# Gate projection as one level of Strassen's product over pairs of token tiles

## The chip, the cores and the metric

One core of one Trainium2 chip runs the whole layer in a single launch. The metric is device microseconds (us) of one execution; lower is better. Times of a kernel are medians of several executions.

## The reference, cut to what matters

One encoder layer over 1024 tokens with model width 1024. After the two attention branches the reference ends like this:

```python
y = jnp.einsum('bse,ed->bsd', jnp.concatenate([ya, yb], axis=-1), w_out[i])
x = x + y
gate = jax.nn.sigmoid(jnp.einsum('bsd,de->bse', x, w_ple_gate[i]))
x = x + gate * jnp.einsum('bsp,pd->bsd', p[i], w_ple_proj[i])
```

The product with `w_ple_gate` (1024 x 1024 by 1024 x 1024) is the gate product; it is the last matrix product of the kernel. Every float32 operand of a large product is split into a high and a low part, and a product is the sum of three matmuls: high by high, high by low, low by high.

## The kernel before, in words

**Tiling.** Tokens come in 8 tiles of 128 rows. A tile of `x1` (the residual stream after the output projection) is 128 x 1024. Matmuls are 128x128 stationary by 128x512 moving. The work of each engine is issued in the order of the program text; every engine and the DMA queue of SyncE (SP, all loads and stores of this part) work strictly in that order.

**The end of the attention and the output projection.** The loop over `i` (lines 1339 to 1383) runs the differential attention; its last turns are i = 33 to 37. `outb` (line 1015) adds branch B's share of the output projection and stores it to DRAM as `xpd`. `outa(t)` (line 1219) loads tile t of `xpd`, makes 24 matmuls into a two-bank PSUM tile, and VectorE adds the two (line 1233). `outa(0)` to `outa(4)` are issued in turns 33 to 37 (line 1330), `outa(5)` to `outa(7)` in the loop behind (lines 1384 to 1395). Between them lies the rest of the attention for the last query pair (pair 15): `d_f` and `d_f2` (lines 1159 to 1175: one VectorE operation, then six short ones on GpSimd), `d_fb` (line 1177, transposes on TensorE, behind `outa(4)`), `d_y` (line 1185: VectorE line 1190, ScalarE line 1195, GpSimd line 1196).

**The gate.** `load_wg` and `split_wg` (lines 1203 to 1214) load and split the weights, 8 rows of 128x1024, once. For each token tile `x1_trans` (line 1236) transposes the tile on TensorE (8 transposes), and ScalarE and VectorE make the two parts. `gate(t)` (line 1249) makes 48 matmuls, 24 for each half of 512 columns; then a tanh on ScalarE (line 1263), two VectorE operations (lines 1264, 1265) and a store. The gate runs one tile behind the transposes, and the last three `outa` are threaded between the first gates.

**Buffers.** SBUF pools: `T8` (16 of 8 KB), `T4` (8 of 4 KB), `TA` (6 of 4 KB), `T2`/`T15` (11 of 2 KB). PSUM has 8 banks: `PS` hands out 4 single banks, `PS2` two tiles of two banks. A new tile waits until all readers of the tile that had its buffer are done.

Of the kernel before, what the change touches and what calls it, by code (L numbers as in the profile page):

```python
# [15 lines left out]
P = 128  # L16
D = 1024
# [23 lines left out]
def layer_kernel(ctx, tc, x, p, ngr, w_in, w_out, gains, lamv, t5p, rpbp, w_gate, w_ple,  # L41
                 onehot, pen, sel, out):
    nc = tc.nc
# [95 lines left out]
    idn = CT([P, P], n="idn")  # L139
# [148 lines left out]
    ppd = [DT([P, D], n="ppd") for _ in range(8)]  # L288
# [388 lines left out]
    pts = {}  # L677
# [282 lines left out]
    for i in range(len(steps) + 2):  # L960
# [8 lines left out]
        if got:  # L969
            n, t0, c = got  # L970
# [31 lines left out]
    xpd = [DT([P, D], n="xpd") for _ in range(8)]  # L1002
# [196 lines left out]
    wgh = []
    wgl = []  # L1200
    wgr = {}

    def load_wg(kc):
        wgr[kc] = T4([P, D], n="wgr")
        ld(wgr[kc], w_gate[kc * P:(kc + 1) * P, :])

    def split_wg(kc):
        if kc % 2 == 0:
            wgh.append(T8([P, 2, D], F32R, n="wgh"))
            wgl.append(T8([P, 2, D], F32R, n="wgl"))  # L1210
        r = wgr.pop(kc)
        h, l = wgh[kc // 2], wgl[kc // 2]
        act(h[:, kc % 2], r, AF.Copy)
        zl.append(lambda: V.tensor_tensor(l[:, kc % 2], r, h.bitcast(F32)[:, kc % 2], op=OP.subtract))
# [21 lines left out]
    def x1_trans(t):
        xt = x1[t]
        h = T4([P, 8, P], F32R, n="x1h")
        l = T4([P, 8, P], F32R, n="x1l")
        for g in range(2):  # L1240
            tp = PS([P, 4, P], "x1p")
            for k in range(4):
                kc = 4 * g + k
                nc.tensor.transpose(tp[:, k], xt[:, kc * P:(kc + 1) * P], idn)
            act(h[:, 4 * g:4 * g + 4], tp, AF.Copy)
            V.tensor_tensor(l[:, 4 * g:4 * g + 4], tp, h.bitcast(F32)[:, 4 * g:4 * g + 4], op=OP.subtract)
        x1T[t] = (h, l)

    def gate(t):
        h, l = x1T.pop(t)  # L1250
        xt = x1.pop(t)
        for c in range(2):
            cs = slice(c * 512, c * 512 + 512)
            pp = T2([P, 512], n="ppl")
            ld(pp, ppd[t][:, cs])
            ps = PS([P, 512], "gps")
            for k in range(8):
                wh, wl = wgh[k // 2][:, k % 2, cs], wgl[k // 2][:, k % 2, cs]
                mm(ps, h[:, k], wh, start=(k == 0), stop=False)  # L1259
                mm(ps, h[:, k], wl, start=False, stop=False)  # L1260
                mm(ps, l[:, k], wh, start=False, stop=(k == 7))  # L1261
            th = T2([P, 512], n="gth")
            act(th, ps, AF.Tanh, scale=0.5)
            V.scalar_tensor_tensor(th, th, 1.0, pp, op0=OP.add, op1=OP.mult)
            V.tensor_tensor(xt[:, cs], th, xt[:, cs], op=OP.add)
            ld(out[t * P:(t + 1) * P, cs], xt[:, cs])
# [72 lines left out]
    for i in range(1, NI + 6):  # L1339
        pre_d(i)  # L1340
        if i == 1 or i == 2:
            load_wout(1, i + 1)
        if i == 28 or i == 31:
            for k in range(2):
                load_wout(0, k + 2 * (i == 31))
        even = i % 2 == 0
        pv = (i - 4) // 2
        if even and i < NI:
            load_u(i // 2)
        for m in range(2):  # L1350
            if i < NI:
                d_e(i, m)
            if 0 <= i - 3 + m < NI:
                d_l(i - 3 + m, 1 - m)
            if m == 0 and 0 < i <= NI:
                d_a(i - 1)
            if even:
                if 0 <= (i - 6) // 2 < NP and m == 0:
                    d_f((i - 6) // 2)
                    d_f2((i - 6) // 2)  # L1360
                filler(i, m)
                if 0 <= pv < NP:
                    d_pv(pv, 4 * m)
            else:
                if 0 <= (i - 7) // 2 < NP and m == 1:
                    d_y((i - 7) // 2)
                if 0 <= (i - 5) // 2 < NP and m == 0:
                    d_pv2((i - 5) // 2)
                filler(i, m)
            if i + 1 < NI:  # L1370
                d_s(i + 1, m)
            if 0 <= i - 2 < NI:
                d_t(i - 2, m)
            if not even and m == 0 and 0 <= (i - 7) // 2 < NP:
# [4 lines left out]
        if i >= 34:
            for kc in (2 * (i - 34), 2 * (i - 34) + 1):  # L1380
                load_wg(kc)
                if i > 34:
                    split_wg(kc - 2)
    for t in range(5, 8 + 6):
        z_low()
        if t == 5:
            split_wg(6)
            z_low()
            split_wg(7)
        if 0 <= t - 5 < 8:  # L1390
            x1_trans(t - 5)
        if t >= 6:
            gate(t - 6)
        if t < 8:
            outa(t)
# [63 lines left out]
```

## Time and profile before

| what | value |
|---|---|
| median of 3 executions | 829.63 us (827.16 to 831.23) |
| the profiled execution, own time | 825.45 us |
| its span in the profile | 823.7 us |
| TensorE (PE) busy | 781.7 us, 95% of the span |
| VectorE (DVE), ScalarE (ACT), GpSimd (POOL) busy | 514.6, 437.2, 261.3 us |
| mean granted TensorE clock | 0.984 of full |

The span runs from the first to the last instruction of the profiled execution; 1.75 us of that execution's time lie around it. PE is the matmul pipe, PEld the weight loads that overlap it, SPq the queue of SyncE. Matmuls overlap in the pipe, so that the time between two starts (not the 390 ns of one) is what a matmul costs.

### The profile page before, as it was taken

Reading aid. Unit: us, or ns where it says so; the run is one execution under the profiler, and the core shown is the slowest. Engines: PE = TensorE matmul, PEld = TensorE weight load, DVE = VectorE, ACT = ScalarE, POOL = GpSimd, SP = SyncE. Lnnn points to the kernel's source line nnn. Section 1 sums busy time; section 2 is a strip of 40 time slices with the busy share of each in tenths; the row PEclk is TensorE's granted clock in tenths of the full one; section 3 lists DMA queues with packets and bytes.
Section 4 is the critical chain, followed back from the end, with each engine's and each line's share of the span. In section 5 each row is a group of like instructions: output and inputs, shape, how many; then the busy total and the mean of one; then the engine's idle time right before and its main releaser. Section 6 shows DMA issues by size and latency. Waiting matters only on the chain.

```text
span 823.7 us, 12188 instructions
## 1 busy us (share of the span) xinstructions
PE 781.7 (95%) x4242; PEld 647.9 (79%) x4242; DVE 514.6 (62%) x990; ACT 437.2 (53%) x814; POOL 261.3 (32%) x263
## 2 busy tenths in 40 slices
PE   7999899999989999797989988999999999999997
PEld 6788688888878887576867867888888877888886
DVE  4658976786997675445536568777777743732332
ACT  5765545254444545335635578888888852311120
POOL 1001433352655400011101035777777752100000
PEclk9999999999999999999989999999999999999999
DMA  8855363862889997585767578667577427122222
GB/s 318 321 199 185 120 212 101 283 156 85 237 262 239 239 307 198 142 232 164 213 174 194 168 219 231 169 173 209 162 211 192 161 96 281 77 89 91 93 87 90
DMA packets 118541, 151.94 MB, mean 184 GB/s; under 512 B 23848, under 2 KB 76744, under 8 KB 118352
## 3 DMA queue, kind: packets, MB, share of 16 engines
q1 hardware_dynamic: 116688, 145.39, 58.9%
q0 software_dynamic: 1792, 5.77, 2.1%
q8 instruction: 34, 0.56, 0.3%
q14 instruction: 27, 0.22, 0.1%
HBM read 104.96 MB, written 46.17 MB: 183 GB/s over the span
## 4 chain that ended last, share of the span: by engine, by line
PE 65%; DMA 11%; DVE 11%; ACT 5%; issue 3%; SPq 3%; POOL 2%; DVEq 0%; ACTq 0%; POOLq 0%
PE dsp L1066 6%; PE ips L234 6%; PE ips L236 6%; PE ips L235 6%; PE gps L1261 4%; PE gps L1259 4%; PE gps L1260 4%; DMA Vw<-vb 3%; PE dtp L1108 3%; SPq L97 2%; PE ntp L685 2%; DMA wraw<-in_w_in_dram 2%; PE dpv L1135 2%; PE zps L582 2%; PE zps L584 2%
## 5 line engine op out<-in xcount | busy, mean ns | idle before, releaser
L234 PE MATMUL ips<-w,xh 128*128 128x512 f32 x336 | 134.0, 399 | 3.6 <-DVE C L260 3.0
L236 PE MATMUL ips<-w,xl 128*128 128x512 f32 x336 | 131.8, 392 | 0.0
L235 PE MATMUL ips<-w,xh 128*128 128x512 f32 x336 | 131.3, 391 | 0.0
L1091 POOL TENSOR_TENSOR s<-s,s 128x1024 f32<-128x1024 f32 x32 | 77.1, 2408 | 57.0 <-ACT s L1090 55.3
L433 POOL TENSOR_TENSOR qrs<-qms,nhalf 128x16 f32<-128x16 f32 x16 | 51.4, 3214 | 91.1 <-DVE qms L431 91.1
L1076 DVE CUSTOM_DVE_ANT_0 s<-dsp,T 128x1024 f32<-128x1024 f32 x64 | 77.7, 1215 | 2.5 <-PE dsp L1066 2.5
L234 PEld LDWEIGHTS ips<-w,xh 128*128 128x128 f32 x336 | 63.4, 189 | 17.1 <-issue 3.8
L1078 ACT ACTIVATE s<-s,dm 128x1024 f32<-128x1024 f32 x64 | 73.3, 1146 | 4.6 <-DVE dm L1076 4.5
L1066 PE MATMUL dsp<-K,Q 128*128 128x512 f32 x256 | 69.7, 394 | 4.9 <-DVE dm L1076 4.3
L236 PEld LDWEIGHTS ips<-w,xl 128*128 128x128 f32 x336 | 63.4, 189 | 13.8
L1115 DVE TENSOR_TENSOR aTl<-dtp,aTh 128x512 fp32r<-128x512 f32 x64 | 44.2, 691 | 48.0 <-ACT aTh L1109 48.0
L235 PEld LDWEIGHTS ips<-w,xh 128*128 128x128 f32 x336 | 63.6, 189 | 12.7
L716 POOL TENSOR_TENSOR yb<-nay,yb 128x128 fp32r<-128x128 f32 x32 | 16.4, 514 | 168.8 <-ACT yb L715 168.8
L218 DVE TENSOR_TENSOR w<-wraw,w 128x512 fp32r<-128x512 f32 x84 | 62.2, 778 | 5.6 <-ACT w L217 5.5
L687 ACT ACTIVATE PT<-ntp 96x768 f32<-96x768 f32 (+1 forms) x32 | 25.9, 810 | 63.0 <-PE ntp L685 63.0
L1066 PEld LDWEIGHTS dsp<-K,Q 128*128 128x128 f32 x256 | 45.9, 189 | 14.6 <-issue 3.1
L582 PE MATMUL zps<-xh,zw 128*128 128x512 f32 x128 | 54.2, 423 | 0.0
L584 PE MATMUL zps<-xh,zw 128*128 128x512 f32 x128 | 51.3, 401 | 0.0
L583 PE MATMUL zps<-xl,zw 128*128 128x512 f32 x128 | 51.1, 399 | 0.0
L217 ACT ACTIVATE w<-wraw 128x512 fp32r<-128x512 f32 x84 | 48.4, 626 | 4.7 <-DVE wraw L193 4.7
L1109 ACT ACTIVATE aTh<-dtp 128x512 fp32r<-128x512 f32 x64 | 38.0, 593 | 23.8 <-PE dtp L1108 23.7
L1259 PE MATMUL gps<-wgh,x1h 128*128 128x512 f32 x128 | 50.5, 395 | 0.0
(177 smaller groups left out, 1820.9 us busy)
## 6 DMA issues: line engine op xcount, KB each, us to landing
wraw<-in_w_in_dram SPq DMA_DIRECT2D x72, 256.0 KB
x<-in_x_dram SPq DMA_DIRECT2D x8, 512.0 KB
ppd<-pp SPq DMA_DIRECT2D x8, 512.0 KB
K<-kbh SPq DMA_DIRECT2D x8, 512.0 KB
Q<-qbh SPq DMA_DIRECT2D x16, 256.0 KB
Q<-qah SPq DMA_DIRECT2D x16, 256.0 KB
Q<-qal SPq DMA_DIRECT2D x16, 256.0 KB
wor<-in_w_out_dram SPq DMA_DIRECT2D x8, 512.0 KB
```

Of the source, the lines that this page charges most:

```text
L218: V.tensor_tensor(w[:, 1], r, w.bitcast(F32)[:, 0], op=OP.subtract)
L234: mm(ps, lh[:, k, a:a + P], w[:, 0], start=(new and k == 0), stop=False, skip_group_check=cont)
L235: mm(ps, lh[:, k, a:a + P], w[:, 1], start=False, stop=False, skip_group_check=cont)
L236: mm(ps, ll[:, k, a:a + P], w[:, 0], start=False, stop=(k == 3), skip_group_check=cont)
L433: G.tensor_tensor(rs, ms, nhalf, op=OP.pow)
L582: mm(ps, w[:, 0, kc], xh(kc, a, b), start=(kc == 0), stop=False)
L584: mm(ps, w[:, 1, kc], xh(kc, a, b), start=False, stop=(kc == 7))
L1066: mm(ps[:, cs], q[g][:, m, u * P:(u + 1) * P], k[:, cs], start=(g == 0), stop=(g == 1))
L1076: V.tensor_tensor_reduce(out=s, in0=ps, in1=back(Td[h][:, :], 1919 - (896 - P * qt), [[-1, S]]), scale=-1.0, scalar=BIG, op0=OP.add, op1=O ...
L1078: act(s, s, AF.Exp, bias=mx, scale=-1.0, accum_out=z[:, m:m + 1])
L1091: G.tensor_tensor(s1, s1, s2, op=OP.add)
L1259: mm(ps, h[:, k], wh, start=(k == 0), stop=False)
```

## The change

The gate product is computed for pairs of token tiles (p, p + 4) as a 2 x 2 block product with seven products in place of eight (the Winograd form of Strassen). The four quarters of the weights give seven right operands: B11, B21, B22 and the sums T1 to T4; the two token tiles give seven left operands: A11, A12, A22 and S1 to S4. Products P1, P6, P7, P4 accumulate in one PSUM bank (A), P5 and P3 in another (B), P2 in a third (C), and partial sums are copied out between them. In detail:

- `gate(p)` makes 7 products of 12 matmuls for two tiles. Tile pair 0's transposes and splits (`g_left1` to `g_left3`) stand between the last three `outa`; pair p + 1's stand inside `gate(p)`.
- `g_first(k)` makes T1, T2 by two GpSimd subtractions for each of four rows k and splits B11, B21, T1, T2; it is issued at the ends of turns 35, 36, 37 and behind `outa(5)`. `g_second(k)` loads the quarters a second time and makes T3, T4 and B22's split; rows 0 and 1 are issued before the first gate, rows 2 and 3 (`extra(0)`) inside it behind P2, the split of T4 (`extra(1)`) behind P7.
- `outa(t)` loads the next tile's `xpd` before its own matmuls and now stores its sum back to `xpd`, one product late; only tiles 0 and 4 stay in SBUF, the others are loaded again in `gate`, and each half tile once more as the addend.
- The last three `outa` run ahead of the first gate.

```diff
...
+    GLEFT = dict(P1="A11", P2="A12", P6="S2", P5="S1", P7="S3", P3="S4", P4="A22")
+    GRIGHT = dict(P1="B11", P2="B21", P6="T2", P5="T1", P7="T3", P3="B22", P4="T4")
...
+    def g_split(n, k, r):
+        h, l = gw[n]
+        act(h[:, k], r, AF.Copy)
+        V.tensor_tensor(l[:, k], r, h.bitcast(F32)[:, k], op=OP.subtract)
+
+    def g_first(k):
+        a, b, c, d = [gr.pop((n, k)) for n in ("B11", "B12", "B21", "B22")]
+        G.tensor_tensor(b, b, a, op=OP.subtract)
+        g_split("B11", k, a)
+        g_split("B21", k, c)
+        G.tensor_tensor(d, d, b, op=OP.subtract)
+        g_split("T1", k, b)
+        g_split("T2", k, d)
+
+    def g_second(k):
+        a, b, c, d = [gr.pop((n, k)) for n in ("B11", "B12", "B21", "B22")]
+        V.tensor_tensor(b, d, b, op=OP.subtract)
+        g_split("T3", k, b)
+        G.tensor_tensor(a, a, b, op=OP.add)
+        G.tensor_tensor(c, c, a, op=OP.subtract)
+        g_split("B22", k, d)
+        gr["T4", k] = c
...
     def outa(t):
-        xt = TA([P, D], n="x1")
-        ld(xt, xpd[t])
+        if t not in oax:
+            outa_load(t)
+        xt = oax.pop(t)
+        if t < 7:
+            outa_load(t + 1)
+        flush()
         pss = PS2([P, D], "oap")
...
         V.tensor_tensor(xt, pss, xt, op=OP.add)
-        x1[t] = xt
...
+        late.append(lambda: st(xpd[t], xt))
+        if t % 4 == 0:
+            x1[t] = xt
...
+    def l_split(p, n, src):
+        w = T4([P, 2, 4, P], F32R, n="x1s")
+        gl[p, n] = w
+        act(w[:, 0], src, AF.Copy)
+        V.tensor_tensor(w[:, 1], src, w.bitcast(F32)[:, 0], op=OP.subtract)
+
+    def g_left1(p):
+        pa, pb = [PS2([P, 2, 4, P], "x1p") for _ in range(2)]
+        pts = [pa[:, 0], pa[:, 1], pb[:, 0], pb[:, 1]]
+        for i in range(4):
+            xt = x1[p + 4 * (i // 2)]
             for k in range(4):
...
+                kc = 4 * (i % 2) + k
+                nc.tensor.transpose(pts[i][:, k], xt[:, kc * P:(kc + 1) * P], idn)
...
+        act(f[:, 0], pts[0], AF.Copy)
+        act(f[:, 1], pts[1], AF.Copy)
+        act(e[:, 0], pts[2], AF.Copy)
+        V.tensor_tensor(e[:, 1], pts[3], e[:, 0], op=OP.add)
+        l_split(p, "A22", pts[3])
+        l_split(p, "A11", f[:, 0])
+        l_split(p, "A12", f[:, 1])
+        V.tensor_tensor(e[:, 0], f[:, 0], e[:, 0], op=OP.subtract)
+        l_split(p, "S1", e[:, 1])
+        V.tensor_tensor(e[:, 1], e[:, 1], f[:, 0], op=OP.subtract)
...
+    def gate(p, extra):
...
+        pre = [g_pre(p, 0), g_pre(q, 1)]
+        g_prod(p, A, "P1", True)
+        act(wv[:, 0], A, AF.Copy)
+        while last:
+            last.pop()()
+        if nxt:
+            x1_load(p + 1)
+            x1_load(q + 1)
+        flush()
+        g_prod(p, C, "P2", True)
+        th = T2([P, 512], n="gth")
+        V.tensor_tensor(th, C, wv[:, 0], op=OP.add)
+        extra(0)
+        g_prod(p, A, "P6", False)
+        act(xy[:, 0], A, AF.Copy)
+        g_fin(p, 0, th, pre.pop(0), th)
+        g_prod(p, B, "P5", True)
+        act(wv[:, 1], B, AF.Copy)
+        if nxt:
+            g_left1(p + 1)
+        pre += [g_pre(p, 1), g_pre(q, 0)]
+        flush()
+        g_prod(p, A, "P7", False)
+        act(xy[:, 1], A, AF.Copy)
+        th1 = T2([P, 512], n="gth")
+        V.tensor_tensor(th1, xy[:, 1], wv[:, 1], op=OP.add)
+        extra(1)
+        g_prod(p, B, "P3", False)
...
+        g_prod(p, A, "P4", False)
...
+        if i == 34:
+            g_load(0, QUARTERS)
+        if i >= 35:
+            if i == 35:
+                g_tiles("B11", "B21", "T1", "T2")
+            g_load(i - 34, QUARTERS)
+            g_first(i - 35)
+    z_low()
+    outa(5)
+    g_first(3)
+    g_left1(0)
+    g_load(0, QUARTERS)
+    outa(6)
+    g_left2(0)
+    g_left3(0)
+    g_load(1, QUARTERS)
+    outa(7)
+    flush()
...
+    def extra(j):
+        if j == 0:
+            g_second(2)
+            g_second(3)
+        else:
+            for k in range(4):
+                g_split("T4", k, gr.pop(("T4", k)))
+
+    g_second(0)
+    g_second(1)
+    for p in range(4):
+        gate(p, extra if p == 0 else lambda j: None)
...
```

In the diff `G` is GpSimd, `V` VectorE, `act` ScalarE. `g_prod` makes the 12 matmuls of a product, `g_pre` loads the two addends of a half tile, `g_fin` is the tanh, the two VectorE operations and a store that is issued late, `flush` issues the stores put off, and `g_left2`, `g_left3` split S2, S3 and S4.

## Rows read from the trace of the kernel before

**Rows 1.** The page, busy time of each engine.
```profile
PE 781.7 (95%) x4242; PEld 647.9 (79%) x4242; DVE 514.6 (62%) x990; ACT 437.2 (53%) x814; POOL 261.3 (32%) x263
```

**Rows 2.** Four stretches: length, busy (instructions) of PE, PEld, DVE, ACT, POOL; clock, DMA share, GB/s.
```profile
681.95:707.66 25.71, 25.71 (x130) 21.76 (x130) 9.90 (x13) 5.83 (x9) 7.84 (x15) 1.00 0.74 286
707.66:715.00 7.34, 7.34 (x43) 6.34 (x42) 5.91 (x7) 5.49 (x8) 0.74 (x1) 1.00 0.00 0
715.00:818.50 103.50, 103.50 (x481) 85.76 (x479) 34.17 (x49) 15.85 (x29) 0.00 (x0) 1.00 0.26 87
818.50:823.70 5.20, 0.00 (x0) 0.00 (x0) 1.38 (x2) 0.60 (x1) 0.00 (x0) 0.73 0.13 50
```

**Rows 3.** The first of the gate's matmul groups by line, 600 us to the end.
```profile
L1259 PE MATMUL gps<-wgh,x1h 128*128 128x512 f32 x128 | 50.5, 395 | 0.0
```

**Rows 4.** ACT in order of time: start, duration, operation, idle before and its releaser.
```profile
795.86 0.60 ACT L1263 ACTIVATE gth<-gps 128x512 f32<-128x512 f32 x1 [4.79 <-PE gps L1261]
796.35 1.09 ACT L1245 ACTIVATE x1h<-x1p 128x512 fp32r<-128x512 f32 x2
802.22 0.60 ACT L1263 ACTIVATE gth<-gps 128x512 f32<-128x512 f32 x1 [4.77 <-PE gps L1261]
807.66 0.60 ACT L1263 ACTIVATE gth<-gps 128x512 f32<-128x512 f32 x1 [4.84 <-PE gps L1261]
```

**Rows 5.** PE in order of time, around `outa(5)`.
```profile
707.66 1.04 PE L1244 MATMUL x1p<-idn,x 128*128 128x128 f32 x8
```

**Rows 6.** DVE and POOL in order of time, durations used for the chain of the change.
```profile
697.18 0.41 DVE L1190 TENSOR_TENSOR y<-oc,dfb 128x256 f32<-128x256 f32 x1
...
684.23 0.19 POOL L1168 TENSOR_TENSOR ft<-ft,drz 128x2 f32<-128x2 f32 x1
686.04 0.19 POOL L1174 TENSOR_TENSOR f<-f,ind 128x2 f32<-128x2 f32 x1
698.12 0.74 POOL L1196 TENSOR_TENSOR yal<-y,yah 128x256 fp32r<-128x256 f32 x1 [11.88 <-ACT yah L1195]
702.47 0.20 POOL L1174 TENSOR_TENSOR f<-f,ind 128x2 f32<-128x2 f32 x1
```

**Rows 7.** DVE and POOL in order of time, 225 to 230 and 249 to 256 us.
```profile
225.37 1.28 DVE L218 TENSOR_TENSOR w<-wraw,w 128x512 fp32r<-128x512 f32 x2
227.77 1.21 DVE L270 TENSOR_TENSOR C<-ips,X 128x1024 f32<-128x1024 f32 x1
251.63 3.46 DVE L218 TENSOR_TENSOR w<-wraw,w 128x512 fp32r<-128x512 f32 x2
...
227.55 2.54 POOL L179 TENSOR_TENSOR wraw<-wraw,wraw 128x512 f32<-128x512 f32 x2
249.33 6.92 POOL L182 TENSOR_TENSOR wraw<-wraw,wraw 128x512 f32<-128x512 f32 x4
```

**Rows 8.** A load of a tile of `xpd`: its issue on SP, and the DVE operation that waited.
```profile
730.20 0.32 SPq L97 DMA_DIRECT2D x<-xpd  x1
733.78 1.22 DVE L1233 TENSOR_TENSOR x<-oap,x 128x1024 f32<-128x1024 f32 x1 [5.70 <-DMA x<-xpd]
```

**Rows 9.** Stretches around three idle times of PE (columns as rows 2), and their ends.
```profile
418.00:430.00 12.00, 7.92 (x42) 6.31 (x39) 4.75 (x17) 2.51 (x7) 0.91 (x2) 0.72 0.56 167
660.00:668.00 8.00, 6.41 (x34) 5.76 (x34) 4.51 (x8) 6.80 (x10) 5.21 (x4) 0.79 0.25 88
679.00:683.00 4.00, 2.73 (x17) 2.14 (x16) 2.15 (x3) 1.21 (x3) 0.72 (x2) 1.00 0.00 1
...
422.26 1.51 PE L685 MATMUL ntp<-idn,nas 128*128 128x128 f32 x6 [4.08 <-DVE nas L675]
662.12 0.61 PE L1156 MATMUL dss<-ones,osq 128*128 128x1 f32 x4 [1.59 <-DVE aTl L1115]
681.48 0.61 PE L1156 MATMUL dss<-ones,osq 128*128 128x1 f32 x4 [1.27 <-DVE aTl L1115]
```

**Rows 10.** The page's second part for 680 to 700 us: GB/s in 40 slices of 0.5 us.
```profile
GB/s 0 0 0 0 0 0 0 0 0 0 287 303 115 377 238 188 426 385 418 442 401 426 401 426 426 418 426 418 418 418 410 418 418 401 401 418 410 410 401 418
```

More of the change, by code (lines that the diff above doesn't have):

```diff
@@ L1196, in d_y @@
         G.tensor_tensor(yl[:, h % 2, cs], y, yh.bitcast(F32)[:, h % 2, cs], op=OP.subtract)
[L1199 to L1214, printed above, removed]
+    GLEFT = dict(P1="A11", P2="A12", P6="S2", P5="S1", P7="S3", P3="S4", P4="A22")
@@ new lines, in layer_kernel, with g_load, g_tiles @@
+    GRIGHT = dict(P1="B11", P2="B21", P6="T2", P5="T1", P7="T3", P3="B22", P4="T4")
+    gw = {}
+    gr = {}
+    gl = {}
+    def g_load(k, names):
+        for n in names:
+            i, j = int(n[1]) - 1, int(n[2]) - 1
+            gr[n, k] = T2([P, 512], n="wgr")
+            ld(gr[n, k], w_gate[(4 * i + k) * P:(4 * i + k + 1) * P, j * 512:(j + 1) * 512])
+    def g_tiles(*names):
+        for n in names:
+            gw[n] = (T8([P, 4, 512], F32R, n="wgh"), T8([P, 4, 512], F32R, n="wgl"))
@@ L1216, in layer_kernel, with flush, outa_load @@
+    QUARTERS = ("B11", "B12", "B21", "B22")
     x1 = {}
     x1T = {}
-    def outa(t):
-        xt = TA([P, D], n="x1")
-        ld(xt, xpd[t])
+    oax = {}
+    late = []
+    def flush():
+        while late:
+            late.pop(0)()
+    def outa_load(t):
+        oax[t] = TA([P, D], n="x1")
+        ld(oax[t], xpd[t])
+    def outa(t):
+        if t not in oax:
[4 more added lines that the diff above has]
+        flush()
         pss = PS2([P, D], "oap")
@@ L1233, in outa @@
         V.tensor_tensor(xt, pss, xt, op=OP.add)
-        x1[t] = xt
[L1236 to L1241, printed above, removed]
-            for k in range(4):
[L1243 to L1266, printed above, removed]
+        late.append(lambda: st(xpd[t], xt))
@@ new lines, in outa, with x1_load @@
+        if t % 4 == 0:
+            x1[t] = xt
+    def x1_load(t):
+        x1[t] = TA([P, D], n="x1")
+        ld(x1[t], xpd[t])
+    lt = {}
+    def l_split(p, n, src):
[8 more added lines that the diff above has]
+            xt = x1[p + 4 * (i // 2)]
+            for k in range(4):
+                kc = 4 * (i % 2) + k
+                nc.tensor.transpose(pts[i][:, k], xt[:, kc * P:(kc + 1) * P], idn)
+        x1.pop(p)
+        x1.pop(p + 4)
+        f = TA([P, 2, 4, P], n="x1f")
+        e = TA([P, 2, 4, P], n="x1e")
+        lt[p] = (f, e)
+        act(f[:, 0], pts[0], AF.Copy)
[8 more added lines that the diff above has]
+        V.tensor_tensor(e[:, 1], e[:, 1], f[:, 0], op=OP.subtract)
@@ new lines, in g_left2, with g_left3, g_prod @@
+    def g_left2(p):
+        f, e = lt[p]
+        l_split(p, "S2", e[:, 1])
+        l_split(p, "S3", e[:, 0])
+        V.tensor_tensor(e[:, 1], f[:, 1], e[:, 1], op=OP.subtract)
+    def g_left3(p):
+        l_split(p, "S4", lt.pop(p)[1][:, 1])
+    def g_prod(p, ps, n, new):
+        w = gl.pop((p, GLEFT[n]))
+        h, l = gw[GRIGHT[n]]
+        c = not new
+        for k in range(4):
+            mm(ps, w[:, 0, k], h[:, k], start=(new and k == 0), stop=False, skip_group_check=c)
+            mm(ps, w[:, 0, k], l[:, k], start=False, stop=False, skip_group_check=c)
+            mm(ps, w[:, 1, k], h[:, k], start=False, stop=(k == 3), skip_group_check=c)
@@ new lines, in g_pre, with g_fin @@
+    def g_pre(t, c):
+        cs = slice(c * 512, c * 512 + 512)
+        pp, xr = T2([P, 512], n="ppl"), T2([P, 512], n="x1r")
+        ld(pp, ppd[t][:, cs])
+        ld(xr, xpd[t][:, cs])
+        return pp, xr
+    def g_fin(t, c, src, pre, th=None):
+        cs = slice(c * 512, c * 512 + 512)
+        pp, xr = pre
+        th = T2([P, 512], n="gth") if th is None else th
+        act(th, src, AF.Tanh, scale=0.5)
+        V.scalar_tensor_tensor(th, th, 1.0, pp, op0=OP.add, op1=OP.mult)
+        V.tensor_tensor(xr, th, xr, op=OP.add)
+        late.append(lambda: ld(out[t * P:(t + 1) * P, cs], xr))
@@ new lines, in layer_kernel @@
+    last = []
+    def gate(p, extra):
+        q = p + 4
+        nxt = p + 1 < 4
+        A, B, C = [PS([P, 512], "gab") for _ in range(3)]
+        wv = TA([P, 2, 512], n="gwv")
+        xy = TA([P, 2, 512], n="gxy")
+        pre = [g_pre(p, 0), g_pre(q, 1)]
[26 more added lines that the diff above has]
+        g_prod(p, B, "P3", False)
+        th2 = T2([P, 512], n="gth")
+        V.tensor_tensor(th2, B, xy[:, 0], op=OP.add)
+        g_fin(q, 1, th1, pre.pop(0), th1)
+        if nxt:
+            g_left2(p + 1)
+        g_prod(p, A, "P4", False)
+        g_fin(p, 1, th2, pre.pop(0), th2)
+        if nxt:
+            g_left3(p + 1)
+        flush()
+        pr = pre.pop(0)
+        last.append(lambda: g_fin(q, 0, A, pr))
@@ L1378, in layer_kernel @@
                 d_ss((i - 5) // 2)
[L1379 to L1395, printed above, removed]
+        if i == 34:
[15 more added lines that the diff above has]
+    outa(7)
+    flush()
+    g_tiles("T3")
+    for k in (2, 3):
+        r = T8([P, 2, D], n="wgr")
+        for i in range(2):
+            ld(r[:, i], w_gate[(4 * i + k) * P:(4 * i + k + 1) * P, :])
+        for n in QUARTERS:
+            gr[n, k] = r[:, int(n[1]) - 1, 512 * (int(n[2]) - 1):512 * int(n[2])]
+    g_tiles("B22", "T4")
+    def extra(j):
[3 more added lines that the diff above has]
+        else:
+            for k in range(4):
+                g_split("T4", k, gr.pop(("T4", k)))
[3 more added lines that the diff above has]
+        gate(p, extra if p == 0 else lambda j: None)
+    while last:
+        last.pop()()
+    flush()
 def _consts():
```

## The prediction

> **What bounds the kernel now.** The page comes first: PE is busy 95% of the span, the next engine, VectorE, 62% [rows 1]. An average hides stages, so the second view is by stretches. From 681.95 us to 818.5 us PE is busy without a gap at full clock, while VectorE works 9.9 of 25.7 us, 5.9 of 7.3 and 34 of 103.5; GpSimd does nothing from 715 on [rows 2]. So the stretch that the change rewrites is pure TensorE time: a matmul less shortens it, and any wait that is added to PE lengthens it. The other engines have room on average, not necessarily in the right order; 5.2 us of tail follow (tanh, two VectorE operations, a store).
>
> **The gain.** The gate has 3 lines of 128 matmuls (lines 1259 to 1261; one stands in rows 3), 384 [rows 3]. The change makes 4 pairs x 7 products x 12 = 336: 48 fewer. Two tanh without transposes between them start 5.44 us apart (802.22 to 807.66) for 24 matmuls, 0.2267 us each; with 8 transposes between, 6.36 us, so 8 transposes cost 0.92 us [rows 4]. Transposes stay 64. Gain: 48 x 0.2267 = **10.9 us**. It must survive what follows.
>
> **What the other engines get.** Before, the weights cost 8 ACT and 8 VectorE operations of 1024 columns and nothing on GpSimd. Now there are 28 splits (28 ACT, 28 VectorE operations of 512), 4 VectorE subtractions and 16 GpSimd ones. Durations: two ACT copies take 1.09, so 0.5 apart and about 0.6 to a reader [rows 4]. Two VectorE subtractions of 512 columns take 1.28 in a row, 0.6 apart; GpSimd needs 1.27 for one [rows 7]. At 249 us both run at once: four GpSimd operations take 6.92 and two VectorE ones 3.46, that is 1.73 for one of each. They take turns; neither runs while the other does. The VectorE operation that reads PSUM at 227.77 keeps its 1.21 us beside GpSimd [rows 7]. All of the new weight work reads two SBUF operands, so I charge turns.
>
> The Trainium skill, "Advanced Engine Details and Errata", section "VectorE Performance Modes", names this blocking for Vector instructions in the modes with two ports, in which it does not list float32 subtraction. By that table alone nothing here would block, and the sum would be that of rival 2 below; rows 7 say otherwise. "GPSIMD Engine Reference", section "8. Key points", adds instructions with two SBUF inputs, with which rows 7 agree.
>
> **Loss 1: between `outa(5)` and `outa(6)`.** `outa(5)` can start at 707.66, when `d_fb` is done [rows 5]; with 24 matmuls and 16 transposes `outa(6)` could start at 707.66 + 5.44 + 1.84 = 714.9. But PSUM has two `PS2` tiles: the second transpose tile needs `outa(5)` added, and `outa(6)` needs the first one copied out by ACT. Both stand in their queues behind `g_first`, and that chain runs over GpSimd:
> - The GpSimd half of pair 14's y ends at 698.86 [rows 6]. `g_first(0)`: two turns with GpSimd (0.6 + 1.25 twice), T2's copy 0.55, its low part 0.65: 703.8.
> - Only then comes VectorE's `d_f` of pair 15, short (two columns), then six GpSimd operations: 2.0 us in one turn (684.23 to 686.23), 3.8 in another (698.86 to 702.67) [rows 6]; I take 2.8: 706.7, just ahead of `d_fb`, which ends at 707.66.
> - `g_first(1)` on GpSimd waits behind these: 2.5 + 0.55 + 0.65: 710.4.
> - The add of `outa(4)` 1.15 (on PE done before 707.66, so it waits for VectorE), with the 1.22 of the add in rows 8 less the overlap, y 0.4, its copy 0.45, its GpSimd part 0.74 [rows 6]: 713.1.
> - `g_first(2)` waits behind that: two turns and a VectorE operation, 4.1: 717.2. T2's low part loses a turn to `g_first(3)`, 1.85: 719.1.
> - The add of `outa(5)`: 720.2, and PE, idle since 714.0, makes the last 8 transposes. `g_first(3)`'s last subtraction ends at 720.4; T2's copy 0.55 and the two copies of the transposes 1.1 bring `outa(6)` to 722.0.
>
> Loss 722.0 - 714.9 = **7.1 us**. Without turns the same chain gives 718.5, a loss of 3.6; with 3.8 for `d_f2` 8.1. Ends 3.6 and 9.
>
> **Loss 2: in the first gate.** Count from the end of `outa(7)`. Free of waits its 84 matmuls and 16 transposes take 84 x 0.2267 + 1.84 = 20.9. VectorE's queue: the add 1.25, rows 0 to 3 of `g_second`, with the sum behind P2 (0.6) between. A row is subtraction, GpSimd, low part, GpSimd, low part: 0.6 + 1.25 + 0.6 + 1.25 + 0.6 = 4.3. Row 3's subtraction ends at 1.25 + 0.6 + 3 x 4.3 + 0.6 = 15.4. ACT's copy of A behind P6 stands behind row 3's two copies: 15.4 + 0.55 + 0.5 + 0.6 = 17.1. P7 writes A and so starts at 17.1, not at 12.7. VectorE leaves row 3 at 19.1; two operations for the first half tile 1.2, seven of `g_left1(1)` 4.2, one sum 0.6, the four low parts of T4 2.4: 27.5, and P4's last two matmuls 0.45 behind: 28.0. Loss 28.0 - 20.9 = **7.1 us**. Without turns it is set by the transposes of pair 1 (12.7, or 14 if their tiles land late), the copies 1.5, then 7.2 of VectorE and 0.45: 1 to 2.6. Ends 1 and 9.
>
> **Clock.** Behind an idle time of 4.08 us the granted clock fell to half (1.2 GHz of 2.4): a mean of 0.72 over 12 us is 6.7 us at half. Behind one of 1.59 us it did too, 0.79 over 8 us or 3.4 us at half; behind one of 1.27 us it did not [rows 9]. At half clock matmuls lose 1.7 to 3.4 us. Loss 1 leaves PE idle for about 6 us, and nothing hides what follows: I take **2.5**. In the first gate VectorE covers it: 0. Ends 0 and 6.
>
> **The rest.** Later gates have no GpSimd work; a pair takes 20.9 us on PE against 22 VectorE operations x 0.6 = 13.2 and 18 on ACT x 0.5. Their tiles are asked for some 5 us after the gate begins and land 3.6 us later [rows 8], by 9 to 11, where the transposes come at 10.9: **0.3**, ends 0 and 2. The DMA queue carries 418 GB/s when full [rows 10]: behind the last `outa` stand 0.5 MB of store, 2 MB of weights, 1 MB of addends and 1 MB of tiles, 11 us, so pair 1's tiles land at 12 to 14, inside loss 2. The loads ahead in `outa` gain nothing, since PE did not wait there. The tail keeps its 5.2 us: four VectorE operations (2.4) fit under P4 (2.7); ends -0.3 and 0.5.
>
> **Sum.** -10.9 + 7.1 + 7.1 + 2.5 + 0.3 = **+6.1 us**. The durations are those of one execution of 825.45 us (span 823.7), 4.2 below the median of 829.63; added to the median: **835.7 us**, 0.7% slower. The ends give 823 to 845.
>
> **Rivals.**
> 1. *The covers hold; faster.* The place is T2's low part of row 2: if it is done before `outa(5)` ends at 713.1, PE waits only for the add (0.5), and if row 3 of `g_second` is done by 12.7 in the first gate, P7 waits for nothing. Price -10.9 + 0.5 + about 0.5: 819.7. For it: from 715 us on VectorE is busy a third of the time [rows 2]. Against: by the queues the two dates are 719 and 19.
> 2. *Long chain, no turns.* -10.9 + 3.6 + 2 + 1.7 + 0.3 = -3.3: 826.3, no change. For it: GpSimd's work here is a subtraction beside subtractions of another length, and parts may miss one another. Against: rows 7.
> 3. *Data late besides.* The second copy of the weights is asked for behind the store of the last tile; if it lands 3 us later than I count, the first gate ends later by as much, and the clock falls again: 840 to 845. For it: 11 us of full DMA [rows 10]. Against: weights stand first in that queue.
>
> That fewer than 48 matmuls go is excluded: the counts stand in the loops.
>
> **Chances.** What a measurement of this kernel can tell from no change is about 0.5%, 4.1 us: faster means below 825.5, slower above 833.8. The forecast has 0.45 (of it 0.07 under 833.8), rival 1 0.23, rival 2 0.23 (0.04 of it under 825.5), rival 3 0.09. Faster 0.23 + 0.04 = 0.27; slower 0.38 + 0.09 = 0.47; within 0.5% 0.26. The likeliest case alone spans 831 to 840. The range for 8 in 10 reaches from rival 1's time, 819, to 842: it leaves out a tenth at each end.
>
> **What would show it.** Right: 336 matmuls in the gate 0.227 apart; PE idle some 6 us behind the first 8 transposes, released by VectorE's add of `outa(5)`, another wait before `outa(6)`, the clock at half after; VectorE subtractions of 1.7 us where GpSimd runs; P7 of the first gate waiting for ACT, P4 for VectorE; later gates 21 us each. Wrong: VectorE and GpSimd at 0.7 and 1.3 us side by side, `outa(6)` within a microsecond of `outa(5)`'s transposes, or a first gate of 21 us.

## The result, and the profile after

The changed kernel takes 842.14 us (median of 4 runs, 840.76 to 842.96), the kernel before beside it 829.07 (4 runs, 827.16 to 831.23): ratio 1.0152, 95% interval 1.0125 to 1.0178. It is 13.1 us **slower**. The forecast was slower by 6.1 us, 835.7; the direction came out, the size by half, and the time lies 0.1 us above the upper end of the range. In this document medians and ratios leave out one far longer execution each of e5 and e8 (955.3 and 4129.8 us) and one of the kernel before (1098.1 us).

The profiled execution took 841.86 us. Its page answers to [rows 1]:

```profile
span 840.1 us, 12365 instructions
...
PE 783.2 (93%) x4194; PEld 645.8 (77%) x4194; DVE 562.0 (67%) x1054; ACT 467.4 (56%) x874; POOL 283.8 (34%) x279
```

48 matmuls are gone, and PE is still busy 1.5 us longer than before: some of its work ran slower. The stretches show where (columns as in [rows 2]). They are: `outa(5)`; the 16 transposes of pair 0; `outa(6)`; `outa(7)`; the four gates; the tail.

```profile
712.28:717.83 5.55, 5.55 (x28) 4.55 (x27) 3.91 (x5) 2.55 (x5) 2.17 (x3) 1.00 0.83 271
717.83:725.94 8.11, 2.65 (x18) 2.36 (x16) 7.82 (x8) 4.53 (x8) 6.26 (x4) 0.85 0.87 310
725.94:733.59 7.65, 7.65 (x27) 6.11 (x25) 5.21 (x9) 3.91 (x7) 0.00 (x0) 0.71 0.49 161
733.59:739.03 5.44, 5.44 (x26) 4.50 (x24) 3.72 (x5) 0.63 (x1) 0.00 (x0) 1.00 0.25 99
739.03:770.53 31.50, 25.87 (x101) 19.99 (x100) 27.68 (x34) 15.07 (x28) 11.61 (x8) 0.85 0.54 195
770.53:792.55 22.02, 21.59 (x101) 17.66 (x100) 12.44 (x21) 9.24 (x17) 0.00 (x0) 0.98 0.54 186
792.55:815.86 23.31, 21.19 (x101) 17.38 (x100) 14.10 (x23) 9.85 (x19) 0.00 (x0) 1.00 0.53 181
815.86:834.90 19.04, 19.04 (x85) 15.58 (x83) 10.82 (x17) 5.92 (x11) 0.00 (x0) 1.00 0.47 165
834.90:840.10 5.20, 0.16 (x1) 0.00 (x0) 2.17 (x4) 0.60 (x1) 0.00 (x0) 0.95 0.40 151
```

The last gate runs free of waits: 84 matmuls in 19.04 us, 0.2267 each. So the gain is there. The losses stand in front of it: 8.11 us for transposes that need 1.84, 7.65 for an `outa` of 5.44, 31.5 for a gate of 20.9. What PE waited for from 640 us on (total, times, longest):

```profile
PE x1p L1298 <- DVE x L1274: 5.5, 1, 5.5
PE dss L1156 <- DVE aTl L1115: 3.0, 2, 1.6
PE x1p L1298 <- DMA x<-xpd: 2.8, 5, 1.6
PE gab L1329 <- ACT gwv L1359: 2.4, 1, 2.4
PE gab L1330 <- DVE wgl L1220: 2.0, 1, 2.0
PE gab L1329 <- ACT wgh L1219: 1.1, 1, 1.1
```

The longest wait is the one forecast, the second half of pair 0's transposes behind VectorE's add of `outa(5)`. PE, VectorE and GpSimd around it, in order of time (start, duration, operation, idle before and its releaser):

```profile
717.83 1.03 PE L1298 MATMUL x1p<-idn,x 128*128 128x128 f32 x8
724.32 1.97 PE L1298 MATMUL x1p<-idn,x 128*128 128x128 f32 x8 [5.46 <-DVE x L1274]
725.94 0.80 PE L1271 MATMUL oap<-woh,yah 128*128 128x512 f32 x1
...
717.30 5.83 DVE L1220 TENSOR_TENSOR wgl<-wgr,wgh 128x512 fp32r<-128x512 f32 x4 [1.00 <-ACT wgh L1219]
723.05 1.21 DVE L1274 TENSOR_TENSOR x<-oap,x 128x1024 f32<-128x1024 f32 x1
724.18 1.28 DVE L1220 TENSOR_TENSOR wgl<-wgr,wgh 128x512 fp32r<-128x512 f32 x2
...
717.51 1.72 POOL L1224 TENSOR_TENSOR wgr<-wgr,wgr 128x512 f32<-128x512 f32 x1
719.31 1.59 POOL L1227 TENSOR_TENSOR wgr<-wgr,wgr 128x512 f32<-128x512 f32 x1
720.86 1.71 POOL L1224 TENSOR_TENSOR wgr<-wgr,wgr 128x512 f32<-128x512 f32 x1
722.65 1.60 POOL L1227 TENSOR_TENSOR wgr<-wgr,wgr 128x512 f32<-128x512 f32 x1
```

VectorE's four low parts of `g_first(2)` take 5.83 us while GpSimd runs four sums; two of `g_first(3)`, with GpSimd done, take 1.28. VectorE works almost without a gap, at less than half its pace, and the add stands behind. `outa(6)` then starts at half clock: 0.71 on average over its 7.65 us. The other wait that was forecast, of `outa(6)` for ACT, isn't there: at half clock the transposes last until ACT's copies are made.

### The profile page after: what moved, and what is told of

It reads as the page before. It is cut to its first block, busy times and chain, and to the rows that moved or that the text cites. A ratio compares the mean times of both kernels' runs of the same rounds, so it can differ in the third digit from the quotient of the medians.

```text
span 840.1 us, 12365 instructions
## 1 busy us (share of the span) xinstructions
PE 783.2 (93%) x4194; PEld 645.8 (77%) x4194; DVE 562.0 (67%) x1054; ACT 467.4 (56%) x874; POOL 283.8 (34%) x279
## 4 chain that ended last, share of the span: by engine, by line
PE 54%; DMA 16%; DVE 15%; issue 5%; ACT 4%; SPq 4%; POOL 2%; DVEq 0%; ACTq 0%; POOLq 0%
DMA Vw<-vb 6%; PE dsp L1066 6%; PE ips L234 5%; PE ips L236 5%; PE ips L235 5%; SPq L97 3%; PE dtp L1108 3%; PE dpv L1135 2%; DMA x<-xpd 2%; PE pps L314 2%; PE dpv L1137 2%; PE dpv L1136 2%; DMA zraw<-in_w_in_dram 2%; DVE wgl L1220 2%; PE obp L1032 2%
## 5 line engine op out<-in xcount | busy, mean ns | idle before, releaser
L234 PEld LDWEIGHTS ips<-w,xh 128*128 128x128 f32 x336 | 63.1, 188 | 17.1 <-issue 3.8
L1109 ACT ACTIVATE aTh<-dtp 128x512 fp32r<-128x512 f32 x64 | 38.1, 595 | 23.7 <-PE dtp L1108 23.7
L1329 PE MATMUL gab<-wgh,x1s 128*128 128x512 f32 x112 | 45.6, 407 | 3.4 <-ACT gwv L1359 2.4
```

What stands on the lines that cost most here:

```text
L234: mm(ps, lh[:, k, a:a + P], w[:, 0], start=(new and k == 0), stop=False, skip_group_check=cont)
```

## The experiments

The two theories of the first runs: **G**, GpSimd's sums and VectorE take turns, and that makes the queues late; **Q** (later **O**), the order in the queues makes them late, whichever engine sums. One line for each kernel, from its profiled execution in us: the 16 transposes of pair 0 (1.84 without a wait), `outa(6)` (5.44), and the first three gates (20.9 each).

| kernel | median | ratio to before, 95% interval | transposes | outa(6) | gate 0 | gate 1 | gate 2 |
|---|---|---|---|---|---|---|---|
| changed | 842.14 | 1.0152 [1.0125, 1.0178] | 8.1 | 7.7 | 31.5 | 22.0 | 23.3 |
| e1 | 833.76 | 1.0052 [1.0030, 1.0074] | 2.3 | 5.6 | 28.3 | 26.3 | 23.7 |
| e2 | 839.16 | 1.0118 [1.0065, 1.0171] | 5.7 | 7.2 | 28.2 | 27.7 | 22.3 |
| e3 | 840.61 | 1.0135 [1.0098, 1.0172] | 8.2 | 5.6 | 29.3 | 23.2 | 24.0 |
| e4 | 833.85 | 1.0072 [1.0041, 1.0102] | 8.1 | 7.5 | 29.2 | 20.8 | 20.8 |
| e5 | 834.03 | 1.0068 [1.0049, 1.0086] | 8.1 | 7.4 | 29.1 | 20.8 | 20.8 |
| e6 | 829.91 | 1.0016 [1.0000, 1.0032] | 2.5 | 5.6 | 32.1 | 20.9 | 20.8 |
| e7 | 835.48 | 1.0080 [1.0054, 1.0107] | 2.5 | 5.6 | 20.8 | 30.7 | 25.0 |
| e8, and again e11 | 821.13, 821.35 | 0.9908 [0.9880, 0.9937], 0.9913 [0.9893, 0.9932] | 2.5 | 5.6 | 21.0 | 23.1 | 20.8 |
| e9 | 827.46 | 0.9990 [0.9973, 1.0006] | 8.4 | 7.2 | 20.8 | 22.2 | 20.8 |
| e10 | 823.02 | 0.9939 [0.9919, 0.9960] | 2.5 | 5.6 | 22.9 | 22.7 | 20.8 |

The stages in the row of e8 are those of e11, the same kernel.

**e1: GpSimd's sums cut to two columns.** All four sums of `g_first` and `g_second`:
```diff
-        G.tensor_tensor(b, b, a, op=OP.subtract)
+        G.tensor_tensor(b[:, 0:2], b[:, 0:2], a[:, 0:2], op=OP.subtract)
```


> Leaves out part of the computation: the 16 GpSimd sums of the weights are made on 2 of 512 columns; their place in every queue and all waits stay. Theory G (GpSimd's time, its turns with VectorE included, stands in the chain of both losses): the wait before the second half of pair 0's transposes falls from 5.5 us to under 1, outa(6) runs at full clock (5.4 us instead of 7.65), the first gate falls from 31.5 us to about 22.6. Sum 6 + 2 + 9 = 17 us less than the changed kernel: about 825 us. Rival Q (the order of the queues alone makes the waits; VectorE and ACT have as many operations as before): no more than 5 us less, 837 or above.

Measured 833.76. Loss 1 is gone whole (2.3 and 5.6 us), as G has it. But the time lies between the two theories, and the first gate (28.3 us) far above the 22.6 of G: the waits are now for data.

```profile
PE x1p L1298 <- DMA x<-xpd: 9.2, 4, 3.6
...
PE x1p L1298 <- DVE x L1274: 0.4, 1, 0.4
```

The transposes of the next pairs wait 9.2 us for their tiles, a wait that came out when the one in front of it went. The edit takes away GpSimd's time and its turns together; it does not part the two.

**e2: the same sums, whole, on VectorE** (`G.` to `V.` in the four lines).

> The same 16 sums made by VectorE instead of GpSimd; nothing left out. Theory G: a row of the second set costs VectorE five operations in a row, 3.0 us, instead of 4.3 with turns, and the chain over GpSimd's queue (pair 15's six short operations, its part of y) no longer carries weights: outa(6) about 3 us earlier with 1 us of clock, the first gate about 23.2 us instead of 31.5, together some 12.5 us less: about 830 us. Rival Q: VectorE is the bound of both places and gets 16 operations more, so 5 to 8 us more than the changed kernel: 847 to 850.

Measured 839.16, between the two. The add of `outa(5)` now comes 0.4 us behind PE, but `outa(6)` waits on:

```profile
PE x1p L1298 <- DMA x<-xpd: 5.5, 5, 3.9
...
PE oap L1271 <- ACT x1f L1305: 2.9, 1, 2.9
...
PE x1p L1298 <- DVE x L1274: 0.6, 1, 0.6
```

ACT's copies of the transposes stand behind T2's copy of `g_first(3)`, as the forecast's chain had it. So the first wait of loss 1 goes with GpSimd's sums. The second is one of order: it is there when another engine is slow to make T2, and gone in e1, where the order is the same and the sum short.

**e3: PE kept busy in its waits** by 44 matmuls into a PSUM tile that nothing reads, at the three places:
```diff
+            if p == 0 and i == 2:
+                dummy(22)
...
+        if p == 0:
+            dummy(9)
...
+            dummy(13)
```


> Adds dummy matmuls into a spare PSUM bank: 22 before the second half of pair 0's transposes, 9 ahead of P6 and 13 ahead of P4 of the first gate, where PE waits; no wait is changed. If the clock is a loss of its own: outa(6) 5.4 us instead of 7.65 (2.2 less); in the first gate the slow P6 is hidden by VectorE and gives nothing, P4 follows VectorE's low parts of T4 at full clock (2 to 2.5 less) and P1 of the next gate 0.4: together 4 to 5 us less, 837 to 838. If the clock is hidden everywhere behind the waits: 842, no change.

Measured 840.61, some 3 us short of what was hoped. `outa(6)` is at full clock (5.6, -2.1) with the same wait before it, and the first gate 2.2 shorter, all of it in P4; P6 at full clock gave nothing, as expected. Gates 1 and 2 give back 1.8; transposes now wait longer for tiles (6.2 us in all, 2.8 in the changed kernel). The clock is a loss of its own, but what it gives back meets the next wait.

**e4: tiles of pairs 2 and 3 over GpSimd's queue.**
```diff
-        ld(x1[t], xpd[t])
+        (stp if t % 4 > 1 else ld)(x1[t], xpd[t])
```


> The tiles of pairs 2 and 3 are loaded over GpSimd's DMA queue, which is idle then, instead of SP's, where they stand behind the stores of the gate before. Theory S (the loads are late because SP waits for VectorE's last sums): the waits before the transposes in gates 1 and 2 go (22.0 and 23.3 us to about 20.9): 3.3 us less, about 838.8. Rival D (the data are slow on the way, 8 us from issue to landing): under 1 us less.

Measured 833.85, below both. Gates 1 and 2 are free of waits. Why those tiles were late in the changed kernel stands in SP's queue there, and in the chain of waits:

```profile
759.35 13.50 SPq L97 DMA_DIRECT2D out_dram<-x1r  x3
...
774.85 0.85 SPq L97 DMA_DIRECT2D x<-xpd  x2
```

```profile
775.28 8.06 DMA x<-xpd
```

SP issues in order. For 13.5 us it stands in three output stores of gate 0, each waiting for VectorE; the loads for gate 1's transposes come behind them, 4.3 us after the gate began, and land 8.06 us later, not 3.6. Of the 7.5 us between the two profiled spans (840.1 and 832.6) these gates hold 3.7, which is what the edit aims at. The rest is clock: 1.6 in `outa(1)`, which here ran at full clock, and 2.3 in the first gate, where P4 did so too, behind the same wait for VectorE (1.99 us). Why the clock held there stays open.

**e5: order alone**, on e4: `g_left1(0)` ahead of `g_first(3)`, and the copies wv0, xy0, wv1 ahead of the weights in gate 0.
```diff
     outa(5)
-    g_first(3)
     g_left1(0)
+    g_first(3)
```


> The changed kernel with the tiles of later pairs on GpSimd's queue, as in e4_tiles_on_gpsimd_queue, and only the order of work altered: the transposes of pair 0 and their copies stand ahead of g_first(3), and in the first gate ACT's copies of the accumulators (wv0, xy0, wv1) stand ahead of the weights' copies that follow them. All sums stay on GpSimd. Theory G (GpSimd's sums and VectorE take turns, so the work ahead of the transposes lasts too long whatever follows it): VectorE's add of outa(5) stands behind the low parts of g_first(2), which this leaves where they are, and GpSimd goes on to the sums of k=3 at once; the transposes still take over 7 us instead of 1.8, the first gate gains 2 to 3 us at P6 and little behind it: 831 to 833. Theory O (order is what cost it, since ACT and VectorE work in program order): the 16 transposes come down to about 3 us, outa(6) runs at full clock, the first gate comes to some 24 us: 822 to 825. Before: about 829.

Measured 834.03, no different from e4, and a little above theory G's 831 to 833. Loss 1 stands whole, as G said: the add waits behind `g_first(2)`, and that is slow by turns. In gate 0 the wait at P6 went, and another of 4.3 us took its place (the transposes of pair 1, for tiles).

**e6: sums on VectorE and the order together**, tiles of pair 1 loaded ahead of `outa(7)` over GpSimd's queue.
```diff
+    x1_load(1)
+    x1_load(5)
     flush()
+    g_sub(1)
```


> All that the runs so far point to, in one kernel: the eight sums of g_first and of g_second on VectorE, the order of e5_order_alone, the T3 differences of k=0 and 1 already during outa(6) and outa(7), those of k=2 and 3 taken in pairs so that VectorE never waits for ACT's copy, all x1 tiles of later pairs loaded over GpSimd's queue and those of pair 1 already ahead of outa(7). If the account holds (loss 1 is turns, the first gate is ACT's and VectorE's order plus turns, later gates are SP's queue), the transposes take 2 to 3 us, outa(6) 5.5, the first gate 21 to 23.5 (VectorE has some 35 us of work in the 35 us up to its end, so a wait of 1 to 2 us at P7 or P4 may stay), the others 20.9 each: 818 to 822, ratio 0.987 to 0.993. Rival B (VectorE becomes the bound, as the 3.95 us per row in e2_sums_on_vector hint): waits move to P4 of the first gate and P1 of the second, first gate over 26: 825 or more. Before: about 829.

Measured 829.91: a miss. Loss 1 and the tile waits are gone, and the first gate, 32.1 us, is longer than ever. Its waits, and in order of time SP's queue at its start with a VectorE operation that waited:

```profile
PE gab L1329 <- ACT gxy L1384: 4.4, 1, 4.4
PE gab L1330 <- DVE wgl L1220: 3.3, 2, 2.3
```

```profile
730.76 5.26 SPq L100 DMA_DIRECT2D xpd<-x  x2
736.07 2.26 SPq L97 DMA_DIRECT2D wgr<-in_w_gate_dram  x4
...
744.75 0.69 DVE L1232 TENSOR_TENSOR wgr<-wgr 128x512 f32<-128x512 f32 x1 [1.80 <-DMA wgr<-in_w_gate_dram]
```

The last weights are asked for 5.4 us after PE began the gate (730.65), behind the store of a tile that VectorE had still to add; P4 waits for xy1's copy, which I had left on ACT behind pair 1's.

**e7: those places put right** (loads ahead of `flush()`, xy1 ahead, T3 and B22 ahead of the T4 sums).
```diff
+    for k in (2, 3):
+        r = T8([P, 2, D], n="wgr")
...
     flush()
     g_sub(1)
```


> e6_vector_sums_and_order with its first gate put right where its trace showed waits: the loads of the gate's weights for k=2 and 3 are asked for ahead of the stores of x6 and x7, for which SP stood 5.3 us until VectorE had added; ACT's copy xy1, for which P4 waited 4.4 us, stands ahead of the copies of pair 1's transposes; the parts of T3 and B22 for k=2 and 3 stand ahead of the T4 sums, and the copies A11 and A12 ahead of A22. If those places are the whole of the 11.2 us that the first gate still took above 20.9, it comes to 21.5 to 23 and the run to 819 to 821, ratio 0.988 to 0.991. Rival B (VectorE's amount of work is the bound, whatever its order: in e6 it was busy 34.9 of the 40 us from 720 to 760): the first gate stays above 26 and the second begins with a wait for A11: 824 or more. Before: about 828.5.

Measured 835.48, rival B's side by the time, not by its reason: the first gate took 20.8 us. But wv0, for which P6 of gates 1 to 3 waits, now stood on ACT behind the copy for S4, which waits for VectorE (PE's waits, then ACT in order of time):

```profile
PE gab L1333 <- ACT gwv L1363: 10.8, 3, 6.3
```

```profile
762.72 0.63 ACT L1288 ACTIVATE x1s<-x1e 128x512 fp32r<-128x512 f32 x1 [1.79 <-DVE x1e L1323]
763.26 0.58 ACT L1363 ACTIVATE gwv<-gab 128x512 f32<-128x512 f32 x1
```

**e8: wv0 ahead** of the left parts S4 and A22, which move into the next gate (only this move is shown; the others are named in the expectation).
```diff
         act(wv[:, 0], A, AF.Copy)
         extra(0)
+        if p:
+            g_left3(p)
```


> e7_gate0_reordered had its first gate at 20.8 us and lost 14 us in the later ones, where ACT's copy of the first accumulator (wv0, for which P6 waits) stood behind ACT's copy for S4, which waited for VectorE. Here S4's and A22's copies follow wv0 in the next gate, the left parts are made in the order in which the products use them, the transposes' copies of pairs 2 and 3 stand behind P5 as in the changed kernel, and two of the first gate's outputs are finished after the second gate's wv0. If waits in ACT's order are all that is left, every gate takes 20.8 to 22 and the run 818 to 820.5, ratio 0.987 to 0.990. Rival B (VectorE is behind with its work at the end of the first gate and something waits for it wherever it is put): the second gate takes over 24: 822 or more. Before: about 828.

Measured 821.13, and 821.35 when run again for its profile:

> The kernel of e8_second_gate_too again, for a profile of it: its six times fell in two groups, 818.7 to 819.2 and 823.1 to 823.7, and e10_t4_sums_on_gpsimd, which differs by the engine of the eight T4 sums, gave 823.0 with 22.9 us in its first gate. If the T4 sums on GpSimd are what costs e10 its 2 us there, this profile shows a first gate of 20.8 to 21.5 us, a second of 21 to 22, and a time under 822, ratio 0.988 to 0.992. If the upper group is the rule (a half clock during outa(1), or a wait that e10 shares), 823 and the same waits as in e10. Before: about 828.5.

Both beat the kernel before; by the second, 0.9% (6.9 us). That is a little short of what e8 was to give, and nearer to it than to rival B: gate 1 takes 23.1 us, where 22 and over 24 were expected. From the start of `outa(5)` (713.31) to the end of the span (821.9) it needs 108.6 us, against 116.0 before (707.66 to 823.7). What is left of waits there: 0.6 us before the transposes and 1.3 in the gates; gate 1 still takes 2.2 too long. e10, below, has 22.9 in its first gate against 21.0 here, 1.9 us that go with the T4 sums on GpSimd, and 1.6 more from its `outa(1)` at half clock. Why the first six times of e8 fell in two groups stays open.

**e9: GpSimd in that order** (all eight sums of `g_first` and the eight for T4 back on it), and **e10: only T4's sums on it.**

> e8_second_gate_too with the two sums of each T1, T2 row and the two of each T4 row back on GpSimd, nothing else changed: the sums' engine alone, in an order that leaves no other wait. Theory G (GpSimd and VectorE take turns): before the transposes VectorE's four low parts of g_first(2) again last nearly 6 us, the transposes take 7 to 8 us instead of 2.5, outa(6) runs at half clock (+2), and the first gate gets 3 to 6 us longer, since VectorE has no slack there: 8 to 15 us above e8_second_gate_too, 827 to 834. Rival O (in a good order GpSimd takes work off VectorE): within 2 us of it or below.

> e9_gpsimd_in_best_order with only the two sums of each T1, T2 row moved back to VectorE, so that GpSimd keeps the two of each T4 row: against e9 it is loss 1 alone, against e8_second_gate_too the T4 sums alone. If GpSimd's turns cost only where PE waits for VectorE soon after, the transposes take 2.5 us instead of 8.4 and outa(6) 5.5 instead of 7.2, the gates stay at the 20.8, 22 and 20.8 us of e9, and the time is 7 to 8 us under e9: 819 to 820.5, ratio 0.988 to 0.990. Rival (the second gate's end or P4 now comes to be late, since what waited in front is gone and VectorE is no more ahead): 822 or more. Before: about 828.5.

Measured 827.46 and 823.02; e9 is some 6 us above e8, between the 8 to 15 of theory G and the 2 of its rival, and e10 comes out on its rival's side. They differ in the engine of `g_first`'s sums, and the transposes show it, first in e9, then in e10:

```profile
721.03 1.97 PE L1298 MATMUL x1p<-idn,x 128*128 128x128 f32 x8 [5.71 <-DVE x L1274]
```

```profile
717.82 1.09 PE L1298 MATMUL x1p<-idn,x 128*128 128x128 f32 x8 [0.64 <-DVE x L1274]
```

With `outa(6)` that is 15.5 against 8.1 us: loss 1 and its clock, 7.4 us, from that engine alone. Yet the spans differ by only 3.0 us (823.7 and 820.7), the medians by 4.4: 2.6 come back in gates 0 and 1, where VectorE no longer has the lead that the long wait had given it, and 1.6 in `outa(1)` at half clock. In gate 0 of e9 the T4 sums on GpSimd cost nothing (20.8 us), and turns go on all the same (1.1 us for a low part, 0.6 alone); in e10, without that lead, they cost 1.9. Both are far from the 31.5 of the changed kernel: most of loss 2 is order, that of the loads included.

## Why the prediction was right in direction and half in size

Between the two profiled spans lie 16.4 us (840.1 - 823.7). That is 3.3 more than between the medians: the profiled execution of before lay 3.6 under its median.

| term | forecast | traces |
|---|---|---|
| 48 matmuls | -10.9 | -10.9 |
| loss 1, transposes | +7.1 | +6.3 |
| clock behind it | +2.5 | +2.2 |
| loss 2, first gate, at full clock (e3) | +7.1 | +8.4 |
| clock in the first gate | 0 | +2.2 |
| later gates | +0.3 | +3.6 |
| tail | 0 | 0 |
| ahead of `outa(5)` | 0 | +4.6 |
| sum | +6.1 | +16.4 |

- **Gain.** As worked out: 336 matmuls, 0.2267 us each in the last gate.
- **Loss 1.** Right, in mechanism and size. The turns are measured: VectorE 1.46 us on average and GpSimd 1.6 to 1.7 side by side, where [rows 7] gave 1.73 for one of each. e1 and the pair e9, e10 show that GpSimd's sums are the cause; that it is by turns is read from these durations. The second wait in the chain shows once the clock holds: 0.55 us in e3, 2.95 in e2. The Trainium skill, "GPSIMD Engine Reference", section "8. Key points", has GpSimd contend for SBUF with VectorE instructions of two SBUF inputs, and the trace agrees (1.46 us against 0.6). The table of two-port modes in the Trainium skill, "Advanced Engine Details and Errata", section "VectorE Performance Modes", has none for an operation on two tensors, so by it alone nothing would be held up; the measurement decides.
- **Clock behind it.** Right: mean 0.71 over 7.65 us is 4.4 us at half, 2.2 lost; e3 takes it away.
- **Loss 2: the clock in the first gate, set at 0**, is the term that failed; the chain of VectorE came out. Counted from the end of `outa(7)`, at 739.03, row 3's subtraction ended after 15.35 us (forecast 15.4), P7 began at 17.4 (17.1), VectorE left row 3 at 19.0 (19.1) and had T4's low parts at 28.4 (27.5). But P4 ended at 31.5, 3.1 us behind them, not 0.45. P4 waits for VectorE, and behind that wait its last eleven matmuls ran at half clock: 4.85 us, in e3 2.62. "VectorE covers it" was right for P6 only. P6 too waited (2.4 us, for wv0) and ran at half clock (4.45 us against 2.72), but VectorE's queue went on meanwhile: P4's second matmul starts 26.65 us into the gate, and 26.66 in e3, where P6 ran at full clock. For P4 nothing is left that could cover it. The other 1.3 us are VectorE (0.9 late, 0.7 of it one wait for ACT) and P4's matmuls at full clock (0.4). The wait at P6, for wv0 behind the copies of row 1, was not foreseen, and it was luck that it cost nothing. A row's price was right: 4.2 us from one subtraction to the next (740.37 to 744.59), forecast 4.3.

```profile
740.37 0.68 DVE L1233 TENSOR_TENSOR wgr<-wgr,wgr 128x512 f32<-128x512 f32 x1
741.81 2.86 DVE L1220 TENSOR_TENSOR wgl<-wgr,wgh 128x512 fp32r<-128x512 f32 x2 [0.76 <-ACT wgh L1219]
744.59 0.68 DVE L1233 TENSOR_TENSOR wgr<-wgr,wgr 128x512 f32<-128x512 f32 x1
...
753.70 0.68 DVE L1233 TENSOR_TENSOR wgr<-wgr 128x512 f32<-128x512 f32 x1
755.08 2.92 DVE L1220 TENSOR_TENSOR wgl<-wgr,wgh 128x512 fp32r<-128x512 f32 x2 [0.70 <-ACT wgh L1219]
...
745.30 1.15 ACT L1219 ACTIVATE wgh<-wgr 128x512 fp32r<-128x512 f32 x2 [3.01 <-DVE wgr L1233]
746.36 0.58 ACT L1359 ACTIVATE gwv<-gab 128x512 f32<-128x512 f32 x1
...
746.99 0.50 PE L1329 MATMUL gab<-wgh,x1s 128*128 128x512 f32 x1 [2.36 <-ACT gwv L1359]
763.18 0.50 PE L1329 MATMUL gab<-wgh,x1s 128*128 128x512 f32 x1 [1.06 <-ACT wgh L1219]
765.68 0.79 PE L1330 MATMUL gab<-wgl,x1s 128*128 128x512 f32 x1 [1.99 <-DVE wgl L1220]
...
770.53 0.63 PE L1329 MATMUL gab<-wgh,x1s 128*128 128x512 f32 x1
```

The last line is the first matmul of the next gate. The last two of T4's low parts, in the chain of waits, and then P4's second matmul and the next gate's first in e3, whose first gate begins at 739.35:

```profile
766.14 1.29 DVE wgl L1220 x2
```

```profile
766.01 0.50 PE L1338 MATMUL gab<-wgl,x1s 128*128 128x512 f32 x1 [0.66 <-DVE wgl L1220]
...
768.63 0.39 PE L1337 MATMUL gab<-wgh,x1s 128*128 128x512 f32 x1
```

- **Later gates, 0.3.** The issue was forecast well ("some 5 us after the gate begins", 4.3 measured), the landing was not: 8.06 us instead of the 3.6 of [rows 8], a load with a queue to itself. Here two tiles and four addends are asked for at once, because SP had stood in the stores. e4 shows that the queue is the cause: over GpSimd's the same loads land after 3.6 to 4.9 us. That it is the loads beside them that made 8.06 of 3.6 was not tested by itself.
- **Ahead of `outa(5)`, 4.6.** 2.9 us arose before 392 us, where the two kernels are the same: spread of the execution. The other 1.7 is `outa(1)` at half clock behind an idle time of 1.45 us.
- **Rivals.** Rival 1, "the covers hold", fails as the change stands; e8 shows that the products can pay, with 6.9 us of the 10.9 left, once no queue stands in front of PE. Rival 2 falls with the turns. Rival 3's time (840 to 845) is the one measured, but not by its reason: it had the weights late, and nothing in the first gate of the changed kernel waits for them. It is the tiles that come late, in the later gates and, once the other waits are gone, in the first (e1, e5).

Not tried: the late stores and loads ahead without the new products.

## What to carry to other kernels

Where PE is busy without a gap, count a saving in matmuls against the operands it needs, and walk each in-order queue (ACT, VectorE, GpSimd, SP) from the first product to the last: the instruction that frees PSUM or holds the next load goes ahead of work that can wait. Mending one wait uncovers the next: e1, e5, e6 and e7 each removed a wait and met another one product or one gate later, so mend by stages and read the same view again. A wait near the end of a stage can take the clock of the matmuls behind it as well, and nothing covers those (2.2 us in the first gate). Sums moved to GpSimd are not free help where VectorE reads two SBUF operands at that moment; they cost nothing where VectorE had a lead (the first gate of e9), 1.9 us where it had none (e10), and 7.4 us where PE waits behind it.

## What was not expected of the hardware

- The same stretch of the same instructions ran at full or at half clock, and this went with the idle time ahead of it. Before `outa(1)` PE waits for VectorE's `aTl`. In seven profiles (before, e4 to e7, e9, e11) for 0.99 to 1.32 us, and `outa(1)` takes 5.5 to 5.6 us; in five (changed, e1, e2, e3, e10) for 1.45 to 2.19, and it takes 7.15 to 7.16. So a few tenths of a microsecond of wait that differ from one execution to the next can be worth 1.6 us more, and a difference of that size between two profiled spans need not be the edit's.
- A load of 512 KB took 3.6 us to land with a queue to itself [rows 8], and 8.06 with another of its size and four of 256 KB asked for around it; that these are the reason is argued, not tested.
